# Expert stage of a hybrid decoder layer: w_down by rows, the shift on GpSimd, gates as weights, gathers in other PSUM banks, one-hots by comparing

## The chip, the cores and the metric

One core of one Trainium2 chip runs the whole layer as one program. The metric is the device time of an execution in microseconds (us); a kernel's time is the median of its runs.

## What is computed

One post-norm layer for 512 tokens of width 1024: x <- LayerNorm(ALPHA x + (1 + gate) sublayer(modulate(x))), first with a token mixer (sparse attention beside a gated DeltaNet), then with a mixture of experts: 4 groups of 8 experts, top-1 group and top-2 experts inside it. The change lies in the experts:

```python
gates = top_pe / jnp.sum(top_pe, axis=-1, keepdims=True) * top_gp
e_idx = g_idx * EXPERTS_PER_GROUP + e_local
...
def expert_block(args):
    xb, e = args
    hb = jax.nn.silu(xb @ w_gate[e]) * (xb @ w_up[e])
    return hb @ w_down[e]
...
yb = yb * gate_buf[:, None].astype(yb.dtype)
out = jnp.zeros((n_tok + 1, D), yb.dtype).at[tok_buf].add(yb)[:n_tok]
```

All is float32; w_gate and w_up are 1024x512 and w_down 512x1024 for each of 32 experts.

## The kernel before

The mixer, the first LayerNorm and the routing take about the first 760 us; then come the experts, and the second LayerNorm closes. Each expert has 64 slots (tokens beyond that go through an overflow loop, at pair 14), and two experts make a **pair** of 128 rows, one on each 64-column half of TensorE; there are 16 pairs. Four experts (two pairs) share a gather of 256 columns. For each pair p the program does, on TensorE in this order:

- **combs** of the pair before (combine_block, L1186): products of one-hot columns (OT, in `places`) with its weighted rows, hi and lo part, 8 blocks (two halves c of the 1024 columns, four token blocks t). VectorE adds each to the accumulator `acc` (L1195). Banks come from the ring `pa` for odd t, `pb` for even t;
- **gathers** of the next group (gather, L1207), in `pb`, two a pair, between the combs and behind them: normalized rows n_hi + n_lo times the one-hots `O`, 16 products each; ScalarE (L967) and VectorE (L968) empty one half each into `xg`;
- **one-hots** by token (one_hot_t, four transposes OT, L1214, copied by ScalarE) and, for even p, the slots' **gates** gs (place_gates, L1237: the one-hots as weights, the gates' hi and lo part as the other operand);
- **hbT** (turned_rows, L1155): transposes of hb, the product silu(gate) x up that VectorE makes (L1145 eth, L1147 hb) from pwg and pwu;
- **pwg** of the next pair (first_product, L1256), **py** (last_product, L1269), and **pwu** of the next pair. A product of 128x64 weights with 512 columns shows as two instructions in the trace. VectorE weighs py by the gates into ys (L1164); hi and lo part are split off as yh and yl.

Weights come by 1 MB halves: SP issues one load (half, L1110) after the other into a ring of 13 slots, 12 loads a pair, each as soon as the products that read its slot are done. w_gate and w_up come in pieces of 2048 columns (8 KB a partition), w_down as four pieces of 512 columns (2 KB) per half, since a half holds 512 output columns of all rows.

`acc` is rebuilt in pair 0 from n_hi + n_lo (L1500, VectorE, eight operations). The shift ALPHA x b of the first LayerNorm is added in pair 8's combs by 64 small products (L1189). Within a pair `in_turn()` fixes the order of the steps; a scheduler places what it leaves open. In pair 0 of both kernels, the program has pwu of the first expert of the pair ahead of pwg of the first and then of the second expert, before these alternate.

Of the kernel before, what the change touches and what calls it, by code (L numbers as in the profile page):

```python
# [42 lines left out]
BIAS_AT = 7  # L43
# [38 lines left out]
def decoder_layer(ctx: ExitStack, tc: tile.TileContext, A, out, dbg=None):  # L82
# [746 lines left out]
    b1c = const.tile([P, KT], F32, name="b1c")  # L829

    def first_norm_rows():
# [8 lines left out]
        g.tensor_scalar(b1c, lnc[:, 0, 1], ALPHA, None, op0=OP.mult)  # L840
# [74 lines left out]

    lg = lp.tile([P, NT, 8], F32, name="lg")
# [256 lines left out]
    def combine(parts, c, OT, n, last=False, share=False, bias=False):  # L1173

        for t in range(NT):
            combine_block(parts, c, OT, n, t, pmm if last and t % 2 else pb, share, bias)

    def combine_block(parts, c, OT, n, t, bank, share=False, bias=False):

        w = c.stop - c.start  # L1180
        if len(parts) == 1:
            OT = OT.bitcast(F32)
        if True:
            o = bank("comb")
            for i, y in enumerate(parts):
                pe.matmul(o[:, :w], OT[:n, t * P:(t + 1) * P], y, start=(i == 0), stop=(not bias and i == len(parts) - 1))  # L1186
# [15 lines left out]
    def gather(O, n, xg, j):  # L1202
        o = pb("gx", (P, 2, 256))
# [5 lines left out]
        evacuate(xg, o, j, n)  # L1209
# [20 lines left out]
    def place_gates(gi, O):  # L1230

        o = pb("gs", (P, 2, 2, 2))
        r = []
        for c in range(2):
            e = 4 * gi + 2 * c
            for t in range(NT):
                pe.matmul(o[:, c], O[:, t, c * P:c * P + P], gate_hl[:, t, :, e:e + 2], start=(t == 0), stop=(t == NT - 1))  # L1237
        for c in range(2):
            gs = mo.tile([P, 1], F32, name="gsl", bufs=4)
            for x in range(2):  # L1240
                p = slice(64 * x, 64 * x + 64)
# [18 lines left out]
    def last_product(p, hT, c, lo=0, hi=512):  # L1260

        py = pa("py")
        if hi - lo == 512:
            ws = [half(A["w_down"], 2 * p + x, c, "wd").rearrange("p (j c) -> p j c", j=4) for x in range(2)]
        else:
            ws = columns(2 * p, 512 * c + lo, hi - lo)
# [4 lines left out]
        return weighted(py[:, lo:hi], gs_of[p], P, slice(c * 512 + lo, c * 512 + hi))  # L1271
# [18 lines left out]
    def combinations():  # L1290

        def step(parts, c, OT, bias, t):
            return lambda: combine_block(parts, c, OT, P, t, pa if t % 2 else pb, bias=bias)
# [4 lines left out]
    def whole(p):  # L1298
# [6 lines left out]
        def one_hots():  # L1305
            for q in (p,) if p < PAIRS - 2 else (p, p + 1) if p == PAIRS - 2 else ():
                if q not in OTs:
                    OTs[q] = one_hot_t(groups[q // 2][0], q % 2 * P, P)

        def gates():  # L1310
            if gi and p % 2 == 0:
                gs_of[p], gs_of[p + 1] = place_gates(gi, groups[gi][0])
# [11 lines left out]
    def pair(p):  # L1324
# [13 lines left out]
        if q == PAIRS - 1:  # L1338
            todo = None

            def finish(after, last=True):
                if todo:
                    with tc.issue_after(after.ins):
                        combine(*todo, last, last)

            for step in ((p, 0, 0, 512), 0, 1, (p, 1, 0, 512), (q, 0, 0, 256), (q, 0, 256, 512), (q, 1, 0, 256), (q, 1, 256, 512)):
                if step in (0, 1):
                    finish(first_product(q, "wu", step), False)
                    todo = None
                    if step:  # L1350
                        tail_ = room(1, (P, 128))
                        st2.append(tail_[:, :96].rearrange("p (t i s) -> p t i s", t=NT, i=4))
                        small.extend(tail_[:, 96 + 8 * i:104 + 8 * i] for i in range(3))
                        last = turned_rows(rows_of(q), P, True)
                    continue
                a, c, lo, hi = step
                y = last_product(a, last if a == q else hT, c, lo, hi)
                finish(py_done[0], a == q)
                todo = y + (OTs[a], P)
            combine(*todo, True, True)  # L1360
            for c in (slice(0, 512), slice(512, 768), slice(768, 1024)):
                statistics(c)
            return
        for c in range(2):
            with in_turn():
                waiting.append(last_product(p, hT, c) + (OTs[p], p == BIAS_AT))
# [37 lines left out]
    def overflow():  # L1404
# [6 lines left out]
        with tc.For_i(0, n_over, 1) as it:  # L1411
# [17 lines left out]
            gs = mo.tile([P, 1], F32, name="gsl", bufs=4)  # L1429
# [44 lines left out]
    with tc.issue_after(given[0].ins), tc.issue_after(given[1].ins):  # L1474
# [10 lines left out]
        gate_hl = lp.tile([P, NT, 2, E], F32R, name="gate_hl")  # L1485
        v.tensor_copy(gate_hl[:, :, 0], gate)
        v.tensor_tensor(gate_hl[:, :, 1], gate, gate_hl[:, :, 0].bitcast(F32), op=OP.subtract)
    started = first_product(0, "wu", 0)
    places, turn = m1.tile([P, 2048], F32R, name="places", tag="a0"), [1]
    OTs[0] = one_hot_t(groups[0][0], 0, P)  # L1490
    begun = first_product(0, "wu", 1)
    with tc.issue_after(begun.ins):
        gs_of[0], gs_of[1] = place_gates(0, groups[0][0])

    acc = Parts(*[lp.tile([P, 2, D], F32, name="acc", tag=f"acc{i}", bufs=1) for i in range(2)])
    for c in range(2):
# [117 lines left out]
```

## Time and profile before

| | before |
|---|---|
| median of 3 runs | 1295.35 us (1293.23 to 1299.46) |
| profiled execution | 1300.06 us, span 1298.0 us |
| TensorE busy, share of the span | 1197.1 us, 92% |
| VectorE / ScalarE / GpSimd busy | 792.9 / 428.9 / 220.7 us |
| mean granted TensorE clock | 0.97 |
| moved by DMA | 291.85 MB, of it 1 MB loads: 64 wg, 64 wu, 60 wd |

Spans and starts in the rows count from the first instruction. PE is TensorE (PEld its weight loads), DVE VectorE, ACT ScalarE, POOL GpSimd, SP the engine whose queue issues the weight loads. A name such as pwg<-wg,xg means that pwg is written from wg and xg; L1256 is the line. Matmuls overlap their successors, so distances between starts tell more than the durations beside them.

### The profile page before, as it was taken

To read this page: it belongs to the slowest core of one execution; us is meant where nothing else is said; L and a number is where in the kernel's file an instruction comes from. 1 tells how busy PE (TensorE), PEld (TensorE's weight loads), DVE (VectorE), ACT (ScalarE), POOL (GpSimd) and SP (SyncE) were. 2 spreads that over 40 slices of the span, in tenths; PEclk is the share of its full clock that TensorE was granted. 3 is DMA by queue.
4 is the path that set the end of the run, shared out by engine and by line. 5 is a ranking of instruction groups with operands and counts; after the bars stand their busy time and mean duration, and the time that the engine had idled before them with its cause. 6 is when DMAs were issued, how large, how long until landed. Compare 5 with 4: busy or idle time off the path is not lost. (4 is left out here: it accounts for less than half of the span.)

```text
span 1298.0 us, 16536 instructions
## 1 busy us (share of the span) xinstructions
PE 1197.1 (92%) x6186; PEld 807.8 (62%) x6186; DVE 792.9 (61%) x1685; ACT 428.9 (33%) x895; POOL 220.7 (17%) x180
## 2 busy tenths in 40 slices
PE   4988888989899999999999988999999999999894
PEld 2767766767677777788888773544444564554432
DVE  6797897589995756867647765434333433343327
ACT  3454644665555655422223121111111111111112
POOL 4322233233232221000035220000000000000004
PEclk9989988999999999999999888999999999999987
DMA  7624314111211111466634875899999999999692
GB/s 276 245 65 138 107 41 142 50 56 39 78 38 36 63 66 65 163 227 259 239 132 170 324 277 203 318 403 408 408 408 408 408 370 407 408 408 410 248 383 102
DMA packets 98740, 291.85 MB, mean 225 GB/s; under 512 B 19137, under 2 KB 31585, under 8 KB 81762
## 3 DMA queue, kind: packets, MB, share of 16 engines
q1 hardware_dynamic: 81746, 282.47, 57.1%
q10 hardware_dynamic: 16352, 6.16, 2.0%
q0 software_dynamic: 560, 2.14, 0.4%
q8 instruction: 50, 0.82, 0.3%
q14 instruction: 32, 0.26, 0.1%
HBM read 287.05 MB, written 3.70 MB: 224 GB/s over the span
## 5 line engine op out<-in xcount | busy, mean ns | idle before, releaser
L229 PE MATMUL pj<-h_hi,w_hi 128*128 128x512 f32 (+1 forms) x504 | 204.2, 412 | 18.8 <-ACT h_hi L324 11.9
L231 PE MATMUL pj<-h_hi,w_lo 128*128 128x512 f32 (+1 forms) x504 | 205.8, 409 | 4.6 <-POOL w_lo L225 4.1
L230 PE MATMUL pj<-h_lo,w_hi 128*128 128x512 f32 (+1 forms) x504 | 205.9, 409 | 0.0
L225 POOL TENSOR_TENSOR w_lo<-wr,w_hi 128x1024 fp32r<-128x1024 f32 x43 | 109.3, 2544 | 212.8 <-ACT w_hi L224 165.6
L224 ACT ACTIVATE w_hi<-wr 128x1024 fp32r<-128x1024 f32 x85 | 89.7, 1057 | 139.0 <-PE pj L230 94.0
L229 PEld LDWEIGHTS pj<-h_hi,w_hi 128*128 128x128 f32 x504 | 98.2, 195 | 39.7 <-ACT h_hi L324 14.4
L1256 PE MATMUL pwg<-wg,xg 128*64 128x512 f32 x512 | 118.4, 608 | 0.0
L1256 PE MATMUL pwu<-wu,xg 128*64 128x512 f32 x512 | 116.0, 593 | 0.0
L231 PEld LDWEIGHTS pj<-h_hi,w_lo 128*128 128x128 f32 x504 | 98.5, 195 | 24.0 <-POOL w_lo L225 6.4
L230 PEld LDWEIGHTS pj<-h_lo,w_hi 128*128 128x128 f32 x504 | 98.8, 196 | 17.5 <-DVE h_lo L325 1.1
L1269 PE MATMUL py<-wd,hbTs 128*64 128x512 f32 x480 | 105.5, 592 | 0.0
L1193 POOL TENSOR_TENSOR acc<-acc,ad 128x256 f32<-128x256 f32 (+1 forms) x10 | 8.5, 872 | 501.1 <-ACT ad L1192 501.1
L1195 DVE TENSOR_TENSOR acc<-acc,comb 128x512 f32<-128x512 f32 (+1 forms) x126 | 78.0, 662 | 23.3 <-PE comb L1186 18.5
L1256 PEld LDWEIGHTS pwu<-wu,xg 128*64 128x64 f32 x512 | 37.1, 137 | 73.5 <-issue 73.3
L1256 PEld LDWEIGHTS pwg<-wg,xg 128*64 128x64 f32 x512 | 36.8, 140 | 68.3 <-issue 64.5
L1269 PEld LDWEIGHTS py<-wd,hbTs 128*64 128x64 f32 x480 | 34.4, 137 | 68.6 <-issue 68.6
L1145 DVE SCALAR_TENSOR_TENSOR eth<-eth,pwg 128x512 f32<-128x512 f32 x16 | 11.0, 688 | 102.5 <-ACT eth L1144 100.4
L225 DVE TENSOR_TENSOR w_lo<-wr,w_hi 128x1024 fp32r<-128x1024 f32 x42 | 55.7, 1329 | 27.7 <-ACT w_hi L224 26.7
L358 DVE SCALAR_TENSOR_TENSOR cacc<-pad,convw,cacc 128x512 f32<-128x512 f32 x72 | 66.2, 924 | 6.2 <-ACT cacc L356 6.0
L967 ACT ACTIVATE xg<-gx,h2c 128x256 f32<-128x256 f32 x32 | 17.9, 564 | 153.1 <-PE gx L1207 145.3
L1164 DVE SCALAR_TENSOR_TENSOR ys<-py,gsl,gt2r 128x512 f32<-128x512 f32 (+1 forms) x34 | 24.4, 718 | 63.1 <-PE py L1269 63.1
L1186 PE MATMUL comb<-yh,places 128*128 128x512 f32 (+1 forms) x132 | 54.2, 413 | 3.8 <-DVE acc L1195 3.5
(473 smaller groups left out, 2334.3 us busy)
## 6 DMA issues: line engine op xcount, KB each, us to landing
wg<-in_w_gate_dram SPq DMA_DIRECT2D x64, 1024.0 KB, 9.2
wu<-in_w_up_dram SPq DMA_DIRECT2D x64, 1024.0 KB, 14.1
wd<-in_w_down_dram SPq DMA_DIRECT2D x60, 1024.0 KB, 11.4
wr<-in_w_in_dram SPq DMA_DIRECT2D x31, 1024.0 KB, 5.0
wada<-in_w_ada_dram SPq DMA_DIRECT2D x23, 1024.0 KB, 5.5
wr<-in_w_br_dram SPq DMA_DIRECT2D x8, 1024.0 KB, 6.3
gr<-g_rows ACTq DMA_DIRECT2D x16, 256.0 KB, 5.0
wr<-in_w_out_dram SPq DMA_DIRECT2D x4, 1024.0 KB, 4.9
```

The source lines that it names most:

```text
L224: s.activation(hi, raw, AF.Copy)
L225: (lo_eng.pop() if len(lo_eng) > 1 else lo_eng[0]).tensor_tensor(lo, raw, hi.bitcast(F32), op=OP.subtract)
L229: pe.matmul(o, a[0], b[0], start=start, stop=False)
L230: pe.matmul(o, a[0], b[1], start=False, stop=False)
L231: pe.matmul(o, a[1], b[0], start=False, stop=stop)
L358: v.scalar_tensor_tensor(acc, pad[:, i:i + S], convw[:, ct, i:i + 1], acc, op0=OP.mult, op1=OP.add)
L967: x = s.activation(xg[:, j, :n], o[:, 0, :n], AF.Identity, bias=h2c[:, 1, 1, j:j + 1], scale=h2c[:, 1, 0, j:j + 1])
L1164: v.scalar_tensor_tensor(ys[:n, :w], py, gs, gt2r[:n, c], op0=OP.mult, op1=OP.mult)
L1186: pe.matmul(o[:, :w], OT[:n, t * P:(t + 1) * P], y, start=(i == 0), stop=(not bias and i == len(parts) - 1))
L1195: v.tensor_tensor(acc[:, t, c], acc[:, t, c], o[:, :w], op=OP.add)
L1256: done = pe.matmul(o[64 * x:64 * x + 64], xg[:, 4 * i + j, c0 + 64 * x:c0 + 64 * x + 64], ws[x][:, j * FF:(j + 1) * FF], start=(i == 0 and ...
L1269: py_done[0] = pe.matmul(py[64 * x:64 * x + 64, lo:hi], hT[:, j, 64 * x:64 * x + 64], ws[x][:, j, :], start=(j == 0), stop=(j == 3))
```

## The change

1. `half` loads w_down as 2048 columns in one piece like the others, two rows of the output a partition; so `last_products` sums both output halves at once, py[0] and py[1].
2. The shift: GpSimd loads b to all partitions (two DMAs), multiplies it by ALPHA and adds it to `acc` in eight operations of 128x512 before the pairs; the 64 products go.
3. Gates: per group four products with the gates (nine columns: hi and lo part for each of four experts, and the token's number) as weights and the one-hots, 256 columns, as the other operand. ScalarE copies the nine rows into the buffer of eth, two transposes turn them, VectorE makes gates and, for each slot, its token's place.
4. Gathers take banks of `pmm` (which holds pwg and pwu too) instead of `pb`, and ScalarE empties both halves.
5. One-hots by token come from one VectorE comparison, 128x512, of the slots' numbers with the token's place, instead of transposes and a copy.
6. The last pair becomes a function of its own: combs of pair 14, then hbT and the column products.

```diff
-        if name[:2] == "wd":
-            load(t.rearrange("p (j c) -> p j c", j=4),
-                 src[e].rearrange("p (j c) -> p j c", j=4)[:, :, i * 512:(i + 1) * 512])
-        else:
-            load(t, src[e][:, i * 2048:(i + 1) * 2048])
+        load(t, src[e][:, i * 2048:(i + 1) * 2048])
...
-            for j in range(4) if bias else ():
-                k = c.start // P + j
-                pe.matmul(o[:, j * P:(j + 1) * P], b1c[:, k:k + 1].to_broadcast([P, P]), ident, start=False, stop=(j == 3))
...
-        o = pb("gs", (P, 2, 2, 2))
+        o = pb("gs", (9, 2 * P))
+        for t in range(NT):
+            pe.matmul(o, gate_hl[:, t, gi], O[:, t, :], start=(t == 0), stop=(t == NT - 1))
+        rows = mo.tile([P, FF], F32, name="eth", bufs=1)[:9, :2 * P]
+        s.activation(rows, o, AF.Copy)
+        return rows
+    def turned_gates(rows):
+        o = pb("gsT", (P, 2, 9))
+        r = []
         for c in range(2):
-            e = 4 * gi + 2 * c
-            for t in range(NT):
-                pe.matmul(o[:, c], O[:, t, c * P:c * P + P], gate_hl[:, t, :, e:e + 2], start=(t == 0), stop=(t == NT - 1))
+            pe.transpose(o[:, c, :], rows[:, c * P:c * P + P], ident[:9, :9])
...
+    def token_hots(p):
+        OT = places[:, p % 2 * S:(p % 2 + 1) * S]
+        v.tensor_tensor(OT.rearrange("p (t n) -> p t n", t=8), slot_no[:, None, :].to_broadcast([P, 8, SLOTS]),
+                        gs_of[p][:, 1:, None].to_broadcast([P, 8, SLOTS]), op=OP.is_equal)
...
+    def last_products(p, hT):
+        py = [pa("py") for _ in range(2)]
+        for i in range(2):
+            ws = [half(A["w_down"], 2 * p + x, i, "wd").rearrange("p (j c) -> p j c", j=2) for x in range(2)]
+            for j in range(2):
+                for c in range(2):
+                    for x in range(2):
+                        pe.matmul(py[c][64 * x:64 * x + 64], hT[:, 2 * i + j, 64 * x:64 * x + 64],
+                                  ws[x][:, j, 512 * c:512 * c + 512], start=(i == 0 and j == 0), stop=(i == 1 and j == 1))
...
-        gathers = [lambda j=j: gather(nxt[0], 256, nxt[1], j) for j in js]
+        gathers = [lambda j=j: gather(nxt[0], 256, nxt[1], j, pmm) for j in js]
-        steps = combs[:4] + gathers[:1] + combs[4:] + [one_hots] + gathers[1:] + [gates]
+        steps = combs[:4] + gates + gathers[:1] + combs[4:] + turn_gates + gathers[1:]
...
+    b_row = [m2.tile([P, 512], F32, name="ys", bufs=2) for _ in range(2)]
+    for c in range(2):
+        g.dma_start(b_row[c], A["ln"][0][1][c * 512:(c + 1) * 512][None].to_broadcast([P, 512]))
+        g.tensor_scalar(b_row[c], b_row[c], ALPHA, None, op0=OP.mult)
+    for c in range(2):
+        for t in range(NT):
+            x = acc[:, t, c * 512:(c + 1) * 512]
+            g.tensor_tensor(x, x, b_row[c], op=OP.add)
```

How it moves instructions. On TensorE, in pair 3, from the last combs on (gx is the gather, hbT the end of the comb stretch), before:

```order
L1186 MATMUL comb<-yh,places 128x512
L1186 MATMUL comb<-yl,places 128x512
L1214 MATMUL OT<-ident,places 128x128 x4
L1207 MATMUL gx<-O,n_hi 128x256
L1207 MATMUL gx<-O,n_lo 128x256
...
L1155 MATMUL hbT<-ident,hb 128x128 x4
```

and with the change:

```order
L1184 MATMUL comb<-yh,places 128x512
L1184 MATMUL comb<-yl,places 128x512
L1202 MATMUL gx<-O,n_hi 128x256
L1202 MATMUL gx<-O,n_lo 128x256
...
L1153 MATMUL hbT<-ident,hb 128x128 x4
```

The transposes OT are gone from between the combs and the second gather; the rest of an odd pair stands as it was.

On VectorE, in pair 0 (places and O are one-hots, gsl the gates, eth and hb lead to hbT), before:

```order
L973 TENSOR_TENSOR places<-slot_no,pos 128x256 x3
L1500 TENSOR_TENSOR acc<-n_hi,n_lo 128x8x64
L1242 TENSOR_REDUCE gsl<-gs 64x1 x4
L1500 TENSOR_TENSOR acc<-n_hi,n_lo 128x8x64 x3
L1147 SCALAR_TENSOR_TENSOR hb<-eth,pwu 128x512
```

with the change:

```order
L975 TENSOR_TENSOR places<-slot_no,pos 128x256 x3
L1519 TENSOR_TENSOR acc<-n_hi,n_lo 128x8x64 x2
L1243 SCALAR_TENSOR_TENSOR gsl<-gsT,lim 128x8
L1246 TENSOR_REDUCE gsl<-gsT 64x1 x2
...
L1519 TENSOR_TENSOR acc<-n_hi,n_lo 128x8x64 x2
L1143 SCALAR_TENSOR_TENSOR eth<-eth,pwg 128x512
L1253 TENSOR_TENSOR places<-slot_no,gsl 128x512
L1145 SCALAR_TENSOR_TENSOR hb<-eth,pwu 128x512
```

and on GpSimd, between the last n_lo of the LayerNorm and the overflow loop's first instruction, where nothing stood:

```order
L960 TENSOR_TENSOR n_lo<-acc,n_hi 128x8x64 x2
L1522 DMA ys<-in_ln_dram 128x512 x2
L1523 TENSOR_SCALAR ys<-ys 128x512
L1527 TENSOR_TENSOR acc<-acc,ys 128x512
L1523 TENSOR_SCALAR ys<-ys 128x512
L1527 TENSOR_TENSOR acc<-acc,ys 128x512 x7
L1427 TENSOR_LOAD nx
```

eth and the token one-hot moved in between the acc operations and hb (before, eth stood ahead of all the acc operations), and GpSimd's eight additions to acc can run as soon as VectorE has rebuilt a part of it.

On TensorE, in the second half of w_down of pair 13 (the wd with the lower number is the first expert's, the other the second's; the two py of the change are the two output halves), before:

```order
L1269 MATMUL py_9618<-wd_9619,hbTs_9572 64x512
L1269 MATMUL py_9618<-wd_9621,hbTs_9572 64x512
L1269 MATMUL py_9618<-wd_9619,hbTs_9572 64x512
L1269 MATMUL py_9618<-wd_9621,hbTs_9572 64x512
L1269 MATMUL py_9618<-wd_9619,hbTs_9572 64x512
```

with the change:

```order
L1279 MATMUL py_9542<-wd_9556,hbTs_9514 64x512
L1279 MATMUL py_9543<-wd_9556,hbTs_9514 64x512
L1279 MATMUL py_9542<-wd_9558,hbTs_9514 64x512
L1279 MATMUL py_9543<-wd_9558,hbTs_9514 64x512
L1279 MATMUL py_9542<-wd_9556,hbTs_9514 64x512
L1279 MATMUL py_9542<-wd_9558,hbTs_9514 64x512
L1279 MATMUL py_9543<-wd_9556,hbTs_9514 64x512
L1279 MATMUL py_9543<-wd_9558,hbTs_9514 64x512
```

Before, first and second expert alternate; with the change the first expert has two products in a row, then the second. Of the 22 halves of pairs 4 to 14, 16 have it so: the second half of each and the first half of pairs 5, 7, 9, 11 and 13.

## Rows read from the trace of the kernel before

**Rows 1.** Windows: stretch, busy us of each engine (instructions), granted clock, DMA share, GB/s.
```profile
850.00:900.00 50.00, 49.36 (x264) 25.89 (x262) 19.42 (x35) 6.43 (x11) 0.00 (x0) 1.00 1.03 405
1050.00:1100.00 50.00, 49.67 (x259) 22.79 (x260) 16.59 (x30) 7.39 (x13) 0.00 (x0) 1.00 0.97 383
```

**Rows 2.** Waits of SP's queue, 850 to 1230: total us, times, longest.
```profile
SPq L1110 <- PE pwg L1256: 183.3, 24, 18.1
```

**Rows 3.** Waits of all engines in the same stretch.
```profile
PE comb L1186 <- DVE acc L1195: 3.5, 11, 0.3
PEld pwg L1256 <- DMA wu<-in_w_up_dram: 2.6, 10, 0.3
```

**Rows 4.** TensorE's timeline, two pairs: start, us, instruction, idle before and its releaser.
```profile
853.94 0.50 PE L1186 MATMUL comb<-yh,places 128*128 128x512 f32 x1
...
858.50 0.39 PE L1186 MATMUL comb<-yl,places 128*128 128x512 f32 x1
859.22 0.50 PE L1186 MATMUL comb<-yh,places 128*128 128x512 f32 x1 [0.32 <-DVE acc L1195]
...
860.26 0.60 PE L1214 MATMUL OT<-ident,places 128*128 128x128 f32 x4
860.62 0.36 PE L1207 MATMUL gx<-O,n_hi 128*128 128x256 f32 x1
...
862.60 0.95 PE L1237 MATMUL gs<-gate_hl,places 128*128 128x4 f32 x8
...
870.91 7.04 PE L1269 MATMUL py<-wd,hbTs 128*64 128x512 f32 x32
...
914.69 0.50 PE L1186 MATMUL comb<-yh,places 128*128 128x512 f32 x1
```

**Rows 5.** TensorE's timeline, the combs of pair 8, with the shift.
```profile
1036.14 0.50 PE L1186 MATMUL comb<-yh,places 128*128 128x512 f32 x1
...
1037.52 0.48 PE L1186 MATMUL comb<-yh,places 128*128 128x512 f32 x1
```

**Rows 6.** Windows of 4 us: pair 0, then w_down arriving, then w_gate and w_up.
```profile
796.00:800.00 4.00, 0.03 (x1) 0.06 (x1) 3.81 (x4) 0.00 (x0) 0.00 (x0) 0.54 0.00 0
940.00:944.00 4.00, 4.00 (x20) 1.29 (x18) 0.69 (x1) 0.23 (x1) 0.00 (x0) 1.00 1.05 388
952.00:956.00 4.00, 4.00 (x32) 2.98 (x32) 2.83 (x7) 1.69 (x3) 0.00 (x0) 1.00 1.03 424
```

**Rows 7.** TensorE's timeline, pair 0.
```profile
799.97 1.09 PE L1155 MATMUL hbT<-ident,hb 128*128 128x128 f32 x4 [4.86 <-DVE hb L1147]
```

**Rows 8.** VectorE's timeline, pair 0.
```profile
795.83 2.92 DVE L1500 TENSOR_TENSOR acc<-n_hi,n_lo 128x512 f32<-128x512 f32 x3
798.77 1.05 DVE L1147 SCALAR_TENSOR_TENSOR hb<-eth,pwu 128x512 f32<-128x512 f32 x1
```

**Rows 9.** VectorE's timeline, weight splits at 700 us.
```profile
698.51 1.22 DVE L225 TENSOR_TENSOR w_lo<-wr,w_hi 128x1024 fp32r<-128x1024 f32 x1
...
704.87 9.03 DVE L225 TENSOR_TENSOR w_hl<-wr,w_hl 128x1024 fp32r<-128x1024 f32 x4
```

**Rows 10.** GpSimd's timeline, at 700 us, before pair 0, and in the last pair.
```profile
699.82 11.86 POOL L263 TENSOR_TENSOR wr<-wr,g 128x1024 f32<-128x1024 f32 x4 [5.15 <-DVE w_lo L225]
...
768.39 3.07 POOL L962 TENSOR_TENSOR n_lo<-acc,n_hi 128x512 fp32r<-128x512 f32 x2 [0.42 <-ACT n_hi L961]
...
1268.62 2.50 POOL L1193 TENSOR_TENSOR acc<-acc,ad 128x512 f32<-128x512 f32 x2 [497.15 <-ACT ad L1192]
```

**Rows 11.** TensorE's timeline, first products of pairs 0 and 1.
```profile
778.59 0.64 PE L1256 MATMUL pwu<-wu,xg 128*64 128x512 f32 x1
778.85 0.64 PE L1256 MATMUL pwg<-wg,xg 128*64 128x512 f32 x1
```

**Rows 12.** TensorE's timeline, the last pair.
```profile
1263.49 0.66 PE L1155 MATMUL hbT<-ident,hb 128*128 128x128 f32 x4 [1.15 <-DVE hb L1147]
```

**Rows 13.** Costliest groups of the page: busy us, mean ns, idle before.
```profile
L1145 DVE SCALAR_TENSOR_TENSOR eth<-eth,pwg 128x512 f32<-128x512 f32 x16 | 11.0, 688 | 102.5 <-ACT eth L1144 100.4
```

More of the change, by code (lines that the diff above doesn't have):

```diff
@@ L42 @@
 OVER_AT = 7
-BIAS_AT = 7
 ACC_AT = 4
@@ L1171, in weighted, with combine, combine_block @@
         return (yh[:n, :w], yl[:n, :w]), c
-    def combine(parts, c, OT, n, last=False, share=False, bias=False):
+    def combine(parts, c, OT, n, last=False, share=False):
         for t in range(NT):
-            combine_block(parts, c, OT, n, t, pmm if last and t % 2 else pb, share, bias)
-    def combine_block(parts, c, OT, n, t, bank, share=False, bias=False):
+            combine_block(parts, c, OT, n, t, pmm if last and t % 2 else pb, share)
+    def combine_block(parts, c, OT, n, t, bank, share=False):
         w = c.stop - c.start
@@ L1258, in first_product, with last_product @@
         return done
-    def last_product(p, hT, c, lo=0, hi=512):
+    def last_products(p, hT):
[7 more added lines that the diff above has]
+                                  ws[x][:, j, 512 * c:512 * c + 512], start=(i == 0 and j == 0), stop=(i == 1 and j == 1))
+        return [weighted(py[c], gs_of[p][:, 0:1], P, slice(512 * c, 512 * c + 512)) for c in range(2)]
+    def last_product(p, hT, c, lo, hi):
         py = pa("py")
[L1263 to L1266, printed above, removed]
+        ws = columns(2 * p, 512 * c + lo, hi - lo)
         for j in range(4):
@@ L1270, in last_product @@
                           start=(j == 0), stop=(j == 3))
-        return weighted(py[:, lo:hi], gs_of[p], P, slice(c * 512 + lo, c * 512 + hi))
+        return weighted(py[:, lo:hi], gs_of[p][:, 0:1], P, slice(c * 512 + lo, c * 512 + hi))
     gs_of, st2, small = {}, [], []
@@ L1290, in combinations, with step @@
     def combinations():
-        def step(parts, c, OT, bias, t):
-            return lambda: combine_block(parts, c, OT, P, t, pa if t % 2 else pb, bias=bias)
+        def step(parts, c, OT, t):
+            return lambda: combine_block(parts, c, OT, P, t, pa if t % 2 else pb)
         steps = [step(*x, t) for x in waiting for t in range(NT)]
@@ L1303, in whole, with turn_gates @@
         nxt = groups.get(gi + 1)
[L1305 to L1308, printed above, removed]
+        turned = []
         def gates():
-            if gi and p % 2 == 0:
-                gs_of[p], gs_of[p + 1] = place_gates(gi, groups[gi][0])
+            turned.append(place_gates(gi, groups[gi][0]))
+        def turn_gates():
+            gs_of[p], gs_of[p + 1] = turned_gates(turned[0])
         js = () if nxt is None or p == 0 else (0, 2, 4, 6) if p == 1 else (4 * (p % 2), 4 * (p % 2) + 2)
-        gathers = [lambda j=j: gather(nxt[0], 256, nxt[1], j) for j in js]
+        gathers = [lambda j=j: gather(nxt[0], 256, nxt[1], j, pmm) for j in js]
         combs = combinations()
-        steps = combs[:4] + gathers[:1] + combs[4:] + [one_hots] + gathers[1:] + [gates]
+        gates, turn_gates = ([gates], [turn_gates]) if gi and p % 2 == 0 else ([], [])
+        steps = combs[:4] + gates + gathers[:1] + combs[4:] + turn_gates + gathers[1:]
         for f in steps:
@@ L1333, in pair @@
             groups[n] = tokens_of(n)
+        OTs[p] = token_hots(p)
         with in_turn():
@@ L1337, in pair @@
             first_product(q, "wg", 1)
[L1338 to L1366, printed above, removed]
+        with in_turn():
+            waiting.extend(y + (OTs[p],) for y in last_products(p, hT))
         with in_turn():
@@ L1369, in pair, with last_pair @@
             first_product(q, "wu", 1)
+    def last_pair(q):
+        tail_ = room(1, (P, 128))
+        st2.append(tail_[:, :96].rearrange("p (t i s) -> p t i s", t=NT, i=4))
+        small.extend(tail_[:, 96 + 8 * i:104 + 8 * i] for i in range(3))
+        hb = rows_of(q)
+        OTs[q] = token_hots(q)
+        for f in combinations():
+            with in_turn():
+                f()
+        with in_turn():
+            hT = turned_rows(hb, P, True)
+        todo = None
+        for c, lo, hi in ((0, 0, 256), (0, 256, 512), (1, 0, 256), (1, 256, 512)):
+            y = last_product(q, hT, c, lo, hi)
+            if todo:
+                with tc.issue_after(py_done[0].ins):
+                    combine(*todo, True, True)
+            todo = y + (OTs[q], P)
+        combine(*todo, True, True)
+        for c in (slice(0, 512), slice(512, 768), slice(768, 1024)):
+            statistics(c)
     def overflow_list():
```

43 lines of the change are left out of this document (26 added, 17 removed).

## The prediction

> **What bounds the kernel now.** I read four views. First, the windows: in the expert stage TensorE is busy 49.36 of 50 us at full clock while the DMA share stands at 1.03 [rows 1]; both look full, so the other views must say which one gives way. Second, the waits of the queue that issues the weight loads: in 380 us SP stood 183.3 waiting for pwg to release ring slots [rows 2]. A loader that waits for its consumer is ahead of it. Third, TensorE's own waits: 2.6 us in all for a landing, and eleven stops of at most 0.3 us for VectorE's additions [rows 3]. Between 1050 and 1100 the DMA share falls to 0.97, at 383 GB/s, while TensorE stays at 49.67 [rows 1]: the ring was full and the transfers paused for TensorE. So **TensorE is the bound from hbT at 799.97 [rows 7] to hbT at 1263.49 [rows 12]**, and work taken from its program there is time. Fourth, the timeline: two pairs take 914.69 - 853.94 = 60.75 us, 30.4 each [rows 4].
>
> The sums are made against the profiled execution (1300.06 us); it lies 4.7 above the median 1295.35, and I carry the difference over to that.
>
> **The change part by part.**
>
> *One-hots by place.* The four transposes OT stand from 860.26 to 860.62, 0.36 us [rows 4]. They go from pairs 1 to 13: 13 x 0.36 = **-4.7**. The comparison that replaces them is one VectorE operation of 128x512 with two SBUF inputs, 2.92 / 3 = 0.97 us by the nearest row [rows 8]. VectorE is busy 19.42 of 50 us [rows 1], which hides it except in pair 0 (below); uncovered it would cost 13 x 0.97 = 12.6.
>
> *Shift on GpSimd.* In pair 8 a token block takes 1037.52 - 1036.14 = 1.38 us [rows 5]; two blocks without the shift take 860.26 - 859.22 = 1.04, 0.52 each [rows 4]. Eight blocks: 8 x 0.86 = **-6.9**.
>
> *Gathers in other banks.* The second run of combs stops once: 858.50 to 859.22 is 0.72 us, where four products behind the stop take 860.26 - 859.22 = 1.04, 0.26 each, so 0.46 is lost, 0.32 of it idle for VectorE's acc [rows 4]. Two reasons meet there: VectorE had to empty half a gather between two additions, and the combs of even t drew their banks from the ring that the gathers use. Both go. Eleven such stops [rows 3]: 11 x 0.46 = **-5.1**. ScalarE empties the second half of each gather instead; it is busy 6.43 of 50 us [rows 1].
>
> *Gates as weights.* Eight narrow products take 0.95 us [rows 4]. Now there are four of 128x256, 2.0 / 16 = 0.12 each in the gather from 860.62 to 862.60 [rows 4], and two transposes of 0.36 / 4 = 0.09: 0.66, and a little for the two changes of shape. Seven even pairs by 0.1: **-0.7**. The longer chain behind it (ScalarE copy, transposes, VectorE) is hidden by pwg, since gates are first read when py is weighted.
>
> *Last pair.* hbT stood idle 1.15 us for VectorE's hb [rows 12]; combs of pair 14 now stand there: **-1.2**.
>
> *w_down by rows.* A half is one piece of 8 KB a partition instead of four of 2 KB. In a window in which w_down arrived the rate was 388 GB/s, with the 8 KB pieces of w_gate and w_up 424 [rows 6]. A pair of 12 loads needs 4 x 1.049 MB / 388 + 8 x 1.049 MB / 424 = 30.6 us before and 12 x 1.049 / 424 = 29.7 after. TensorE's pair becomes 30.4 - 0.36 - 0.46 - 0.05 = 29.5. So the transfers have little to spare, but a full ring of 13 loads (13 x 2.5 = 32 us of transfer) stands against the 13 x 0.2 = 2.6 us that TensorE gains on them: **0**. The Trainium skill ("DMA: Bandwidth & Descriptors", Why small descriptors are slow) puts a fixed 3 cycles on each packet; an estimate from it lifts w_down by some 3% only, to about 401 GB/s, and the pair would need 30.3. The trace has this very piece size running at 424, and I go by the row; what the page gives lies within the second rival.
>
> *w_down's products.* Two sums are now open at once, and the products come in another order: in 16 of the halves of pairs 4 to 14, two in a row go to the same 64-column half of TensorE, where they alternated throughout. The 16 products of a pair take 32 passes, 7.04 us [rows 4], 0.22 a pass because two run side by side; alone a pass takes 0.44, a product 0.88. The nearest row is in pair 0, where pwu of the first expert stands ahead of pwg of the first and then of the second expert: the second expert's product starts at 778.85, 0.26 after 778.59 and not 0.88, so it went ahead of the one in the way [rows 11]. I take 0.1 a half: **+1.5**, bounds 0 and 16 x 0.26 = 4.2.
>
> *Start of pair 0.* Here the change costs. hbT starts at 799.97 after 4.86 us idle for VectorE's hb [rows 7], which ran at 798.77 behind three acc operations [rows 8]. Two things push it later. (1) The queue: eth (0.69 [rows 13]; its buffer holds the gates' rows until they are turned) and the one-hot (0.97) now stand ahead of hb, and the gates come through a ScalarE copy and two transposes more, about 1.1 with their hand-overs; one acc operation (0.97) less stands behind the gates: +1.8. (2) GpSimd's eight additions run at the same time. At 700 us four GpSimd operations took 11.86 us [rows 10] while VectorE's w_hl took 9.03 / 4 = 2.26 each, against 1.22 alone [rows 9]: with two SBUF inputs each, the engines took turns. An addition of 128x512 alone takes 2.50 / 2 = 1.25 [rows 10]. Between the last place one-hot and hb VectorE has five such operations (four acc, one one-hot). If each lets one addition past: 5 x 1.25 = 6.3, less some 2 of VectorE's idle time around the gates: +4.2. Together **+6.0**; bounds +1.8 (no turns) and 1.8 + 8 x 1.25 = +12 (all eight). The clock is down there already, 0.54 from 796 to 800, with the transfers at 0 GB/s [rows 6], so a longer gap adds no second fall, and the ring stays full. GpSimd's two loads pass an empty queue: n_lo ends at 771.5 [rows 10].
>
> Sum: -4.7 - 6.9 - 5.1 - 0.7 - 1.2 = -18.6; +1.5 + 6.0 = +7.5; net **-11.1**. Profiled 1289.0, median **1284.3**.
>
> **Rivals.**
>
> 1. *GpSimd's additions cost pair 0 nothing, or all.* For nothing: the turns were seen with 128x1024 only, and gates, eth and hb read PSUM. Then -4.2, 1280.1. For all: the additions wait for acc, as hb does. Then +6, 1290.3.
>
> 2. *The transfers become the bound.* With w_down at 388 to 401 GB/s a pair needs 30.3 to 30.6 us against TensorE's 29.5: up to 13 x 1.1 = 14. For: the share of 1.03. Against: SP's 183 us and the 32 us in the ring. If the ring's lead covers half or less, 7 to 14 return: 1291 to 1298.
>
> 3. *The other side: a product on a busy half holds the free half's.* In each of the 16 halves the second expert's product then starts 0.88 late, and again where its own two stand in a row: 0.88 to 1.76 a half, 14 to 28 in place of 1.5. It decides for slower from (11.1 + 1.5 + 6.5) / 16 = 1.2 a half; at 1.76, 1284.3 - 1.5 + 28 = 1311. The Trainium skill ("TensorE: Matmul & The Clock Gate", Step-by-step: what each phase is for) says that matmuls stay in program order and only weight loads are pulled ahead, which taken word for word is this case. Against it: 0.26 instead of 0.88 at 778.85.
>
> 4. *The stop between combs stays*, if acc itself is late and not the gather: 5.1 back, 1289.4.
>
> **Chances.** A measurement of this kernel can tell about 0.5%, 6.5 us, from no change: faster is under 1288.9, slower over 1301.8. Forecast 0.53 (nearly all faster); no turns 0.14 (faster); all eight 0.12 (same; a quarter faster); transfers 0.07 (same); held products 0.06 (slower 0.04); the stop 0.08 (half and half). Faster 0.74, same 0.22, slower 0.04. The range takes in no turns with free products (1284.3 - 4.2 - 1.5 = 1278.6, and a little for the measurement) and single rivals up to 1292; beyond it lie most of transfers and held products.
>
> **What would show it.** Right: no OT and no stop in the pairs, 29.5 from pair to pair, pair 8 like the others, no drop of the rate while w_down arrives, and hbT of pair 0 near 806 with GpSimd's additions between VectorE's. Wrong: TensorE waiting for landings (2); py of a pair over 7.5 us (3); a stop of 0.3 in the combs (4); hbT of pair 0 before 802 or after 809 (1).

## The result and the profile after

| | before | changed |
|---|---|---|
| median, first comparison (4 runs each) | 1294.29 us (1291.58 to 1299.46) | 1275.57 us (1274.67 to 1277.16) |
| median, second comparison (11 and 5 runs, another chip) | 1296.55 us | 1274.28 us (1271.61 to 1277.43) |
| profiled execution | 1300.06 us, span 1298.0 | 1277.16 us, span 1275.5 |

The ratio is 0.9852 (95% interval 0.9819 to 0.9885) in the first comparison and 0.9831 (0.9805 to 0.9857) in the second: faster by 18.7 and 22.3 us where 11.1 had been forecast, and below what the prediction's range took in (down to 1278.6 and a little for the measurement). The two profiled executions differ by 22.9; that of before lay 5.8 us above its median, that of the change 1.6, so about 4 of it is scatter.

The page of the changed kernel, busy time of each engine (us, share of the span, instructions):

```profile
PE 1174.5 (92%) x6042; PEld 803.4 (63%) x6042; DVE 789.2 (62%) x1701; ACT 433.4 (34%) x913; POOL 230.7 (18%) x190
```

TensorE does 22.6 us less, GpSimd 10 more. The two windows of [rows 1]:

```profile
850.00:900.00 50.00, 50.00 (x264) 25.64 (x262) 19.37 (x36) 7.89 (x15) 0.00 (x0) 1.00 1.01 420
1050.00:1100.00 50.00, 50.00 (x265) 27.99 (x262) 21.49 (x39) 8.55 (x16) 0.00 (x0) 1.00 1.01 420
```

TensorE fills both, and the transfers keep 420 to 421 GB/s at a share of 1.01, without the dip to 383 behind pair 8. SP still waits for TensorE (before [rows 2]):

```profile
SPq L1108 <- PE pwg L1267: 147.8, 25, 11.8
```

The margin is thin, though. As an estimate from these rows, the 12 loads of a pair need 12 x 1.049 MB / 421 = 29.9 us, and TensorE takes 58.59 / 2 = 29.3 for a pair (below), so the ring's lead shrinks by 0.6 us with each.

In the timeline, two pairs take 910.83 - 852.24 = 58.59 us (60.75 in [rows 4]); the second run of combs begins at 885.81 and ends without a stop at 887.67, eight products at 0.23, and the gather follows at once, with no OT:

```profile
852.24 0.50 PE L1184 MATMUL comb<-yh,places 128*128 128x512 f32 x1
...
885.81 0.40 PE L1184 MATMUL comb<-yh,places 128*128 128x512 f32 x1
...
887.44 0.39 PE L1184 MATMUL comb<-yl,places 128*128 128x512 f32 x1
887.67 0.28 PE L1202 MATMUL gx<-O,n_hi 128*128 128x256 f32 x1
...
910.83 0.50 PE L1184 MATMUL comb<-yh,places 128*128 128x512 f32 x1
```

Pair 8, where [rows 5] had 1.38 us a token block, is a pair like the others:

```profile
1028.26 0.50 PE L1184 MATMUL comb<-yh,places 128*128 128x512 f32 x1
...
1028.84 0.40 PE L1184 MATMUL comb<-yh,places 128*128 128x512 f32 x1
```

From its start to the next comb, pwu takes 910.83 - 903.87 = 6.96 us in pair 3, where the products of the two experts alternate ahead of it, and 1028.26 - 1021.25 = 7.01 in pair 7, where w_down's products stand in the turned order:

```profile
903.87 7.04 PE L1267 MATMUL pwu<-wu,xg 128*64 128x512 f32 x32
...
1021.25 7.09 PE L1267 MATMUL pwu<-wu,xg 128*64 128x512 f32 x32
```

Pair 0 on TensorE, first gs of the kernel before:

```profile
794.06 1.05 PE L1237 MATMUL gs<-gate_hl,O 128*128 128x4 f32 x8
```

and the same with the change, hbT behind its idle time (before [rows 7]):

```profile
791.52 0.63 PE L1229 MATMUL gs<-O,gate_hl 128*9 128x256 f32 x4
792.61 0.29 PE L1240 MATMUL gsT<-ident,eth 9*128 9x9 f32 x2 [0.46 <-ACT eth L1231]
798.48 1.11 PE L1153 MATMUL hbT<-ident,hb 128*128 128x128 f32 x4 [5.58 <-DVE hb L1145]
```

on VectorE (before [rows 8]):

```profile
786.56 3.89 DVE L1519 TENSOR_TENSOR acc<-n_hi,n_lo 128x512 f32<-128x512 f32 x4
790.29 1.09 DVE L975 TENSOR_TENSOR places<-slot_no,pos 128x256 fp32r<-128x256 f32 x3
791.43 2.04 DVE L1519 TENSOR_TENSOR acc<-n_hi,n_lo 128x512 f32<-128x512 f32 x2
...
794.12 2.00 DVE L1519 TENSOR_TENSOR acc<-n_hi,n_lo 128x512 f32<-128x512 f32 x2
796.16 0.69 DVE L1143 SCALAR_TENSOR_TENSOR eth<-eth,pwg 128x512 f32<-128x512 f32 x1
796.76 0.68 DVE L1253 TENSOR_TENSOR places<-slot_no,gsl 128x512 fp32r<-128x512 f32 x1
797.36 1.06 DVE L1145 SCALAR_TENSOR_TENSOR hb<-eth,pwu 128x512 f32<-128x512 f32 x1
```

and on GpSimd:

```profile
791.89 1.11 POOL L1522 DMA_DIRECT2D ys<-in_ln_dram  x2 [21.63 <-PE gs L1229]
...
797.43 1.27 POOL L1527 TENSOR_TENSOR acc<-acc,ys 128x512 f32<-128x512 f32 x1
...
800.30 9.20 POOL L1527 TENSOR_TENSOR acc<-acc,ys 128x512 f32<-128x512 f32 x7
```

The start of pair 0 went another way than forecast. From the first pwg to hbT of pair 0 it took 798.48 - 772.89 = 25.59 us; before, 799.97 - 774.10 = 25.87. GpSimd's loads of b started at 791.89 only, after 21.63 us idle, and its first addition at 797.43, when VectorE was already at hb.

Below, all kernels are compared by the starts of hbT in the timeline of one profiled execution each, us (hbT 0 is the hbT of pair 0; after_again is a second trace of the changed kernel; the other names are those of the experiments below, which had one execution each where no number of runs is given):

| kernel | first pwg to hbT 0 | hbT 0 to 1 | pair with gates, without | hbT 7 to 8 | hbT 0 to 14 | hbT 14 to 15 |
|---|---|---|---|---|---|---|
| before | 25.87 | 32.68 | 30.75, 29.98 | 37.31 | 435.22 | 28.30 |
| changed | 25.59 | 32.48 | 29.76, 28.90 | 29.83 | 416.38 | 28.28 |
| after_again | 25.60 | 31.41 | 29.76, 28.90 | 29.83 | 415.29 | 27.75 |
| e1_early_shift | 31.02 | 31.60 | 29.76, 28.90 | 29.83 | 415.51 | 27.85 |
| e2_shift_products | 25.59 | 31.52 | 29.76, 28.91 | 36.99 | 422.63 | 27.63 |
| e3_wd_columns | 25.58 | 31.56 | 29.74, 28.87, from hbT 9 on 30.3 to 31.6, 29.8 | 29.75 | 421.08 | 28.94 |
| e4b_bank_old | 25.59 | 33.08 | 31.13, 29.37 | 31.14 | 427.84 | 27.85 |
| e4_gather_old | 25.60 | 32.89 | 31.40, 29.50 | 31.41 | 430.07 | 27.30 |
| e4c_dve_half | 25.59 | 31.40 | 29.76, 28.91 | 29.80 | 415.24 | 27.79 |
| e5_transposes | 26.17 | 31.78 | 30.21, 29.34 | 30.24 | 420.86 | 30.72 |
| e6_before_rows | 25.88 | 34.11 | 30.75, 30.01 | 37.35 | 437.58 | 28.55 |
| e10_hb_first | 19.85 | 34.56 | 29.75, 28.91 | 29.80 | 432.68 | 26.99 |
| e13_four_ahead | 19.85 | 34.56 | 29.76, 28.91 | 29.80 | 419.70 | 28.31 |
| e14_split_rebuild | 21.50 | 31.61 | 29.76, 28.91 | 29.84 | 415.52 | 27.89 |

Pairs repeat to 0.05 us. The stretch from hbT 0 to 1 does not: 32.48 in one execution of the changed kernel, 31.41 in another, as the granted clock recovers sooner or later after the gap. A difference of 1 us there says nothing.

### The profile page after: what moved, and what is told of

Read it like the earlier page. It is cut to its first block, busy times and chain, and to the rows that moved or that the text cites. A ratio compares the mean times of both kernels' runs of the same rounds, so it can differ in the third digit from the quotient of the medians.

```text
span 1275.5 us, 16286 instructions
## 1 busy us (share of the span) xinstructions
PE 1174.5 (92%) x6042; PEld 803.4 (63%) x6042; DVE 789.2 (62%) x1701; ACT 433.4 (34%) x913; POOL 230.7 (18%) x190
## 5 line engine op out<-in xcount | busy, mean ns | idle before, releaser
L1267 PEld LDWEIGHTS pwu<-wu,xg 128*64 128x64 f32 x512 | 47.3, 137 | 62.3 <-issue 60.0
L1188 POOL TENSOR_TENSOR acc<-acc,ad 128x256 f32<-128x256 f32 x8 | 6.0, 775 | 442.9 <-PE comb L1184 439.8
L1279 PEld LDWEIGHTS py<-wd,hbTs 128*64 128x64 f32 x480 | 39.9, 137 | 63.6 <-issue 63.6
L1145 DVE SCALAR_TENSOR_TENSOR hb<-eth,pwu 128x512 f32<-128x512 f32 x16 | 17.2, 1077 | 65.8 <-PE pwu L1267 65.8
```

The source lines that it names most:

```text
L1145: v.scalar_tensor_tensor(hb[:n], th[:n].rearrange("s (p j) -> s j p", j=4), 0.5, pu[:n].rearrange("s (p j) -> s j p", j=4), op0=OP.mult, o ...
L1267: done = pe.matmul(o[64 * x:64 * x + 64], xg[:, 4 * i + j, c0 + 64 * x:c0 + 64 * x + 64], ws[x][:, j * FF:(j + 1) * FF], start=(i == 0 and ...
L1279: pe.matmul(py[c][64 * x:64 * x + 64], hT[:, 2 * i + j, 64 * x:64 * x + 64], ws[x][:, j, 512 * c:512 * c + 512], start=(i == 0 and j == 0) ...
```

## The experiments

**GpSimd's additions early.** Forecast and trace disagreed on pair 0; the question was whether the two engines do not take turns at this size, or only met too late. In place of the shift, GpSimd adds gt2r, a row whose load is issued at 764.01 and lands 7.0 us later.

```diff
-    b_row = [m2.tile([P, 512], F32, name="ys", bufs=2) for _ in range(2)]
...
-            g.tensor_tensor(x, x, b_row[c], op=OP.add)
+            g.tensor_tensor(x, x, gt2r[:, c * 512:(c + 1) * 512], op=OP.add)
```

> The changed kernel, but GpSimd adds gt2r instead of the shift, without the two loads of b and without the two multiplications by ALPHA, so that its eight additions are ready as soon as VectorE has rebuilt a part of acc, while VectorE still has the other parts to do (the output has another row added to it). Theory (turns): pair 0 lost nothing in the changed kernel only because GpSimd's loads of b waited until 791.9 us, so its additions ran from 797.4 on, behind VectorE's acc operations. With them early the two engines take turns: VectorE's acc operations of 128x512 go from 1.0 us to about 1.3 to 2.2 each, and TensorE's idle time before hbT of pair 0 grows from 5.58 to 8 to 11 us. Rival (no turns at 128x512): VectorE's operations stay at 1.0 us and the idle time stays at 5.0 to 6.0 us.

The timeline of this kernel, first VectorE:

```profile
784.44 5.97 DVE L1519 TENSOR_TENSOR acc<-n_hi,n_lo 128x512 f32<-128x512 f32 x4
790.26 3.17 DVE L975 TENSOR_TENSOR places<-slot_no,pos 128x256 fp32r<-128x256 f32 x3
...
795.99 3.21 DVE L1519 TENSOR_TENSOR acc<-n_hi,n_lo 128x512 f32<-128x512 f32 x2
```

GpSimd:

```profile
785.61 7.20 POOL L1523 TENSOR_TENSOR acc<-acc,gt2r 128x512 f32<-128x512 f32 x4 [17.45 <-DVE acc L1519]
```

and TensorE:

```profile
801.80 1.11 PE L1153 MATMUL hbT<-ident,hb 128*128 128x128 f32 x4 [11.01 <-DVE hb L1145]
```

They take turns. Four acc operations of VectorE took 5.97 us where the changed kernel needed 3.89, three place one-hots 3.17 in place of 1.09, the last two acc operations 3.21 in place of 2.00, and four additions of GpSimd 7.20, where seven nearly without company took 9.20. Taken one by one in shorter windows of the same view, VectorE's operations start at 784.44, 785.36, 786.29, 788.25, 790.26 and 791.61, GpSimd's additions at 785.61, 787.43, 789.38 and 791.37: from the first addition on, one operation passes per addition, and an acc operation takes 2.0 us from start to start in place of 0.93. hbT stood idle 11.01 us, 5.4 more. The forecast's +4.2 for the turns was nearly right as a price; what was wrong was the time at which GpSimd starts.

**The shift by products again.** The diff takes back the change's part 2: `bias` in combine_block, and no b_row.

> The changed kernel with the shift added by the 64 products in pair 8's combs as before, and nothing of it on GpSimd. Theory: pair 8 grows by 6.9 us (hbT 7 to hbT 8 from 29.8 to 36.7), the other pairs stay, and hbT of pair 0 still stands idle 5.5 us, since GpSimd's additions came behind hb there. Rival (GpSimd did slow VectorE ahead of hb): the idle time before hbT of pair 0 falls by 1 us or more, to under 4.6.

The step from hbT 7 to hbT 8 grew from 29.83 to 36.99, by 7.16 (forecast 6.9), and hbT of pair 0 stood idle as before:

```profile
793.99 1.11 PE L1156 MATMUL hbT<-ident,hb 128*128 128x128 f32 x4 [5.58 <-DVE hb L1148]
```

So in the changed kernel GpSimd delayed nothing ahead of hb.

**w_down by columns again.**

```diff
-        load(t, src[e][:, i * 2048:(i + 1) * 2048])
+        if name[:2] == "wd":
+            load(t.rearrange("p (j c) -> p j c", j=4),
+                 src[e].rearrange("p (j c) -> p j c", j=4)[:, :, i * 512:(i + 1) * 512])
+        else:
+            load(t, src[e][:, i * 2048:(i + 1) * 2048])
```

> The changed kernel with w_down loaded by columns as before (four pieces of 2 KB a partition, each half one output half), the products of the two experts alternating. Theory (TensorE is the bound, the ring covers the transfers): the rate falls from 421 to about 405 GB/s, a pair needs 30.6 us of transfer against 29.4 of TensorE, but the lead of the ring lasts: hbT of pair 0 to hbT of pair 15 stays at 444.7 us, up to 447. Rival (the transfers bind once TensorE is faster): TensorE waits for landings and the stretch grows by 7 to 14 us, to 452 to 459; then the loads by rows were worth as much as the shorter combs.

Up to hbT 9 the pairs were those of the changed kernel; then pwu, 6.97 us from its start to the next comb until then, took 7.5 to 8.8. TensorE's timeline and one window:

```profile
1109.92 8.02 PE L1271 MATMUL pwu<-wu,xg 128*64 128x512 f32 x32
...
1145.00 3.65 PE L1271 MATMUL pwu<-wu,xg 128*64 128x512 f32 x14 [0.77 <-DMA wu<-in_w_up_dram]
```

```profile
1150.00:1200.00 50.00, 50.00 (x262) 25.04 (x262) 17.42 (x32) 7.92 (x15) 0.00 (x0) 1.00 1.03 406
```

At 406 to 411 GB/s the ring's lead lasts nine pairs, then TensorE waits for w_up behind w_down. As an estimate, a pair's loads need 30.6 to 31.0 us at these rates, 1.3 to 1.7 more than TensorE, so nine pairs used up 11 to 15 us of lead, less than half of the 32 that the prediction put into the ring. The stretch to hbT 14 took 421.08 in place of 415.3 to 416.4: 5 to 6 us. With hbT 14 to 15 it is 450.0, between the two expectations; both were partly right. The loads by rows gain nothing in themselves, but the other parts would have lost about a quarter of their gain without them.

**w_down by rows alone, in the kernel before.** `half` and `last_products` of the change, in the kernel before, pairs 0 to 13.

> The kernel before with w_down loaded by rows and both output halves summed at once, for pairs 0 to 13 (pair 14 keeps its order and its loads by columns), and nothing else of the change. Theory (worth nothing alone, since TensorE takes 30.4 us a pair and transfers by columns 30.6 with a ring's lead): hbT 0 to hbT 14 stays within 1 us of 435.2, the DMA rate follows TensorE. Rival (TensorE already waited for transfers in ways the waits do not show): 3 us or more shorter.

Pair for pair the same as before (30.75 and 30.01), 1297.39 us beside 1297.98, one execution each. The stretch missed the expected 435.2 by 2.4 (437.58); what it has more lies in hbT 0 to 1 and in pair 14. Alone the loads by rows gain nothing.

**Which part removed the stop.** Three kernels move the gathers back, by halves:

```diff
-        gathers = [lambda j=j: gather(nxt[0], 256, nxt[1], j, pmm) for j in js]
+        gathers = [lambda j=j: gather(nxt[0], 256, nxt[1], j) for j in js]
```

puts them into the old banks; e4b_bank_old keeps ScalarE alone behind them, e4_gather_old has both engines. e4c_dve_half keeps the new banks and has VectorE empty the second half:

```diff
-        evacuate(xg, o, j, n, bank is pmm)
+        evacuate(xg, o, j, n, False)
```

> The changed kernel with the gathers back in the banks that the combs of even t use, but still emptied by ScalarE alone. Theory (the bank): the stop of 0.3 us idle in the second run of combs comes back, since a comb waits for the bank that a gather or the comb two before holds; pairs take about 29.9 us instead of 29.4, the stretch from hbT 0 to hbT 15 about 450. Rival (VectorE's share): with VectorE free of the gathers no stop, 444.7.

> The changed kernel with the gathers in the new banks, but VectorE emptying every second half again. Theory (the bank): no stop in the combs, the stretch from hbT 0 to hbT 15 stays within 1 us of 444.7. Rival (VectorE's share): VectorE's additions fall behind the combs, the stop of 0.3 us idle comes back in most pairs, the stretch about 450.

> The changed kernel with the gathers wholly as before: in the banks of the even combs, emptied by ScalarE and VectorE half each. Theory (the bank is the cause, and two engines empty it sooner than one): the stop comes back, but smaller than with ScalarE alone (which cost 1.4 us in odd pairs and 0.45 in even ones): 0.4 to 0.6 us a pair, hbT 0 to hbT 14 from 415.3 to 416.4 to about 422. Rival: the same as with ScalarE alone, 427.

TensorE's waits from 850 to 1195 us (total us, times, longest), first e4b_bank_old, then e4_gather_old:

```profile
PE gx L1202 <- ACT eth L1231: 2.8, 6, 0.5
PE comb L1184 <- ACT xg L967: 2.2, 12, 0.2
```

```profile
PE comb L1184 <- DVE acc L1190: 3.9, 12, 0.3
PE gx L1202 <- ACT eth L1231: 2.8, 6, 0.5
...
PE gx L1202 <- DVE acc L1190: 1.4, 6, 0.2
```

With VectorE's half but the new banks the pairs are those of the changed kernel. In the old banks the stop is back whoever empties them: 0.47 us a pair without gates with ScalarE alone, 0.6 with both. So it was the bank; that VectorE was freed of the gathers is worth nothing in the new banks (28.91 beside 28.90). My expectation that two engines would empty the bank sooner fell: both together cost more. The pairs with gates lose 1.4 to 1.6, since the new gates (gs, gsT) draw on the same ring: the gather behind gs waits for ScalarE's copy and starts 1.09 us after gs in place of 0.47. Gates as weights and gathers in other banks belong together.

**Transposes again.** one_hot_t in place of token_hots, behind the second run of combs.

> The changed kernel with the one-hots by token made by four transposes and a ScalarE copy again. Theory: pairs 1 to 13 take 0.36 us more each by the transposes alone, and up to 0.5 with the slower start of the products behind them: the stretch from hbT 0 to hbT 15 grows from 443 to 444.7 (its scatter at the clock's recovery included) to 449 to 451. Rival (the one-hot on VectorE is what the pairs wait for): it does not grow, since VectorE becomes free of 0.68 us a pair.

Each pair grew by 0.44 us: 0.36 for the transposes and some 0.08 for the slower start of the product behind them. The stretch to hbT 14 grew by 4.5 to 5.6 (13 x 0.44 = 5.7); up to hbT 15 it is 451.6, just above the expected 449 to 451, and the rival fell. hbT 14 to 15 grew by 2.4 to 3, where the last pair's transposes and their copy now stand in the way.

**A faster version.** In the changed kernel hb of pair 0 still ends behind acc, eth and the one-hot. The gates' rows of pair 0 fit into the second one-hot of `places`, empty until then; so eth and hb need not wait for them:

```diff
-        rows = mo.tile([P, FF], F32, name="eth", bufs=1)[:9, :2 * P]
+        rows = places[:9, S:S + 2 * P] if own else mo.tile([P, FF], F32, name="eth", bufs=1)[:9, :2 * P]
...
+        if p == 0:
+            with in_turn(), tc.issue_after(hb_done[0].ins):
+                gs_of[0], gs_of[1] = turned_gates(rows0.bitcast(F32))
```

In the first try all of acc is rebuilt behind hb, and the last group's gates are made in pair 13.

> A try at a faster version of the changed kernel, three edits: the gates' rows of pair 0 go into the still empty second one-hot of places instead of eth's buffer, so that eth and hb of pair 0 need not wait for them; acc is rebuilt behind hb; and the gates of the last group are made in pair 13 instead of behind the overflow loop. Expected if pair 0 waits for VectorE's queue alone: idle before hbT of pair 0 falls from 5.58 us to about 1, with the clock kept up, 5 us or more gained, and 2 to 3 us at pair 14: about 1268. If the transfers hold pwg of pair 1 then, or acc comes too late for the combs of pair 1, as much of it is lost as TensorE waits there.

It took 1279.78 us. hbT 0 came 5.7 us sooner, but pair 14 later; VectorE's timeline there:

```profile
1215.97 0.69 DVE L1255 TENSOR_TENSOR places<-slot_no,gsl 128x512 fp32r<-128x512 f32 x1 [15.18 <-DMA wu<-in_w_up_dram]
```

The order of the scheduler had moved. The source asks for twelve loads for pairs 14 and 15 in both kernels; in the changed kernel four of them, of w_gate, stood ahead of the overflow loop (from 1178.75, the next at 1210.76), now all twelve did (from 1168.20 to 1195.9). The last, issued near 1195.6, landed 19.8 us later, and the loop's entry waited for it. The second try leaves four there:

```diff
-        load_ahead([(nm, 2 * q + x, i) for nm, q, i in seq for x in range(2)][:len(AGAIN) - 1])
+        load_ahead([(nm, 2 * q + x, i) for nm, q, i in seq for x in range(2)][:4])
```

> The try at a faster version again, with one more edit: only the four loads of w_gate go ahead of the overflow loop, since in the first try twelve stood there and the loop waited for all of them to land (15.2 us idle on VectorE until 1216). Expected: idle before hbT of pair 0 stays near 0.6 us, pair 0 gains about 3.5 us over the changed kernel up to hbT of pair 1, and pair 14 no longer waits for landings: hbT 13 to hbT 14 from 45.2 us to 29 to 31, and the time about 1267 to 1271, 5 to 8 us under the changed kernel. If the transfers, which ran at 421 GB/s throughout, are by now the bound for an earlier TensorE, it is 1272 or more.

1273.23 us (6 runs; ratio 0.9824, 0.9798 to 0.9849), which can't be told from the changed kernel, 1274.28 on the same chip:

> The changed kernel once more, unchanged, beside the faster version on the same chip: 1273 to 1278 us. What differs from its first trace is scatter; expected there above all in the stretch from hbT 0 to hbT 1 and from hbT 14 to hbT 15, where the granted clock recovers (32.5 and 28.3 us in the first trace, 31.4 and 27.8 in another kernel with the same work).

Of the 5.7 us of pair 0, 1.3 were given back in pairs 13 and 14, where the gates of the last group now stood (29.82 and 32.20 beside 28.93 and 31.79), and 2 to 3 in pair 1, whose combs stood idle for the weighted rows:

```profile
809.93 0.49 PE L1186 MATMUL comb<-yh,places 128*128 128x512 f32 x1 [1.98 <-ACT yh L1169]
811.12 0.50 PE L1186 MATMUL comb<-yl,places 128*128 128x512 f32 x1 [0.69 <-DVE yl L1170]
```

VectorE made them late, behind six acc operations and four one-hots that took turns with GpSimd's additions:

```profile
792.76 8.60 DVE L1359 TENSOR_TENSOR acc<-n_hi,n_lo 128x512 f32<-128x512 f32 x6
...
802.00 4.89 DVE L975 TENSOR_TENSOR O<-slot_no,pos 128x256 fp32r<-128x256 f32 x4
```

The last try rebuilds only the second half of acc behind hb, and takes the gates of the last group where the changed kernel does:

```diff
+    rebuilt(0)
...
+        if p == 0:
+            with tc.issue_after(hb_done[0].ins):
+                rebuilt(1)
+            shifted()
```

> A last try at a faster version of the changed kernel: as in the two tries before, the gates' rows of pair 0 lie in the empty second one-hot of places so that hb of pair 0 does not wait for them, and four loads go ahead of the overflow loop; but only the second half of acc is rebuilt behind hb, and the gates of the last group are made where the changed kernel makes them. Expected: hbT of pair 0 comes 25.6 - 5.7 = 20 us after the first pwg; the combs of pair 1 wait less for ys than in the try before (2.7 us), so that hbT 0 to hbT 1 takes 31 to 33 us, and hbT 12 to hbT 14 stays at 60.7 us: 4 to 5 us under the changed kernel, 1269 to 1271. If GpSimd's additions, taking turns with VectorE now that both start early, still hold the combs of pair 1, it is no faster than 1273.

```profile
792.32 0.72 PE L1155 MATMUL hbT<-ident,hb 128*128 128x128 f32 x4 [2.24 <-DVE hb L1147]
```

1268.56 us (5 runs; 0.9773 of before, 0.9751 to 0.9795), below the changed kernel's interval of 0.9805 to 0.9857, if on another chip: hbT 0 comes 4.1 us sooner (5.7 were expected) and pair 1 gives nothing back. From the first pwg to the span's end the profiled execution takes 497.5 us, those of the changed kernel 502.6 and 500.9. It beats both kernels.

## Why the prediction was wrong

The direction was right, the size not: 11.1 forecast, 18.7 and 22.3 measured. By its steps:

- *Start of pair 0*: **the step that failed.** It had +6.0 and the trace has -0.3. "GpSimd's two loads pass an empty queue: n_lo ends at 771.5" was read as a start at 771, with the additions ready while VectorE rebuilds acc. But GpSimd's loads waited 21.63 us for TensorE, until 791.89, so the additions ran behind hb, and the turns had nobody to take them with. That GpSimd's queue was free is shown: in e1_early_shift, which needs neither the loads nor their memory, the first addition starts at 785.61, as soon as acc is there. Why the loads waited is read from the program, and no run moves them elsewhere: the tiles `ys`, into which they load, take over memory of early loads of w_up and w_gate, and the last product that reads one of these ends near 791.6. The price of the turns came near: e1_early_shift paid 5.4 us for them, about 1.0 to 1.2 a meeting where the sum had 1.25, and some five meetings. The number was luck in part, since four of them came ahead of the five operations that the sum named. The queue's +1.8 showed as 1.05 (gs to hbT took 799.97 - 794.06 = 5.91 before and 798.48 - 791.52 = 6.96 now), and a gain that I had not counted outweighs it: from the first pwg to gs 18.63 us in place of 19.96, 0.6 of it the four transposes OT that stood there as well, the rest a quicker run of the products around them. My first rival named the outcome (-4.2, 1280) for the wrong reason, that 128x512 takes no turns.
- *One-hots*: 13 x 0.44 = 5.7, forecast 4.7; the product behind the transposes also started slower, which I had not counted.
- *The stop*: 0.5 to 0.6 a pair, forecast 0.46. Of the two reasons named, the bank is the cause and VectorE's share is not.
- *Shift*: 7.2, forecast 6.9.
- *Gates as weights*: forecast -0.7. Pairs with gates gained 0.99, pairs without 1.08, so nothing, or 0.1 a pair lost. Pair 14 gained nothing at all (hbT 13 to 14 took 31.60 before and 31.79 now): behind the overflow loop TensorE stands idle 2.79 us ahead of gsT for ScalarE's copy, which the sum had taken as hidden.
- *Last pair*: from hbT 14 to the span's end it took 28.30 + (1298.0 - 1263.49) = 62.8 before and 28.28 + (1275.5 - 1243.14) = 60.6 now: -2.2, forecast -1.2. Four blocks of combs of pair 14, which stood between the first two column products, now stand ahead of hbT, where TensorE had been idle 1.15 us; the other 1 us was not taken apart.
- *w_down's products*: forecast +1.5. pwu's stretch behind py is 7.01 with the turned order and 6.96 with the alternating one: 0.05 in 11 pairs, 0.55. The other side's price of 14 to 28 us was not paid: by the program's order a product for the free half went ahead in [rows 11], and the turned order cost next to nothing. The Trainium skill ("TensorE: Matmul & The Clock Gate", Step-by-step: what each phase is for) says that matmuls stay in program order. Taken word for word that is the other side's case, and between two column halves these traces do not bear it out.
- *w_down by rows*: 0, which held for the gain. The transfers ran at 420 to 421 GB/s, as the 424 of [rows 6] said; the ring's lead would not have lasted without it, as the second rival said, if at 5 to 6 us and not 7 to 14. The Trainium skill ("DMA: Bandwidth & Descriptors", Why small descriptors are slow) puts about 3 fixed cycles on each packet. By the prediction's estimate from it the rate would have been 12 x 1.049 / 30.3 = 415 GB/s, which the trace's 420 to 421 does not bear out.

Without the +6.0 the sum is -17.1, 1278.3, within a few us of the measurement; the other terms, most of them a little low, make up 3 to 4 more.

## What to carry to other kernels

An operation on an idle engine starts when its memory is free, not when its queue is: before charging it for a meeting with another engine, look up in the program what held its tiles. When two resources are both full, as TensorE and the transfers here, an edit that is worth nothing alone can carry the gain of the others. A stop with two suspects, a bank and an engine, is told apart by moving one at a time.

## What was not expected of the hardware

VectorE and GpSimd take turns on 128x512 operations with two SBUF inputs: while both run, 2.0 us from start to start in place of 0.93 for VectorE, 1.8 to 2.0 in place of 1.31 for GpSimd (e1_early_shift). The entry of the overflow loop waited for the loads in flight: with twelve ahead VectorE stood idle 15.18 us. And the same gap costs a different amount from one execution to the next. Two windows of 4 us from hbT 0 on (columns as in [rows 1]), of the changed kernel:

```profile
798.50:802.50 4.00, 4.00 (x12) 1.70 (x14) 2.50 (x5) 0.60 (x1) 4.00 (x4) 0.50 0.00 0
802.50:806.50 4.00, 4.00 (x16) 1.17 (x14) 0.40 (x1) 0.60 (x1) 4.00 (x4) 0.81 0.15 23
```

and of the same kernel in another execution:

```profile
800.30:804.30 4.00, 4.00 (x14) 1.66 (x16) 2.51 (x5) 0.60 (x1) 4.00 (x4) 0.58 0.00 0
804.30:808.30 4.00, 4.00 (x22) 1.35 (x20) 0.69 (x1) 0.60 (x1) 4.00 (x4) 1.00 0.28 61
```

After the same 5.6 us of idle time the granted clock was at 0.50 and 0.81 in the one and at 0.58 and 1.00 in the other, which is the 1 us between 32.48 and 31.41.
